# Stacked scores in the second attention, and the last output projections token tile by token tile

## The chip, the cores and the metric

The kernel runs on one core of a Trainium2 chip. The metric is the device time of one execution in microseconds, as the median of several runs. The kernel before takes 2476.68 us (three runs, 2473.72 to 2478.02).

A core has a matrix engine (TensorE, PE in the profile, with its weight loads apart as PEld), three engines for elementwise work (VectorE or DVE, ScalarE or ACT, GpSimd or POOL) and SyncE (SP), which here only issues DMAs. Each runs its own queue of instructions in order and waits for the others by semaphores.

## The reference

512 tokens of 1024 features go through two blocks in float32. The first block has a convolution branch, an attention and a feed-forward layer; the change does not touch it. The second block has two layers: one with the second attention, one with a state-space model (SSM), each followed by a feed-forward layer (FFN) with a short convolution. Cut to what the change touches:

```python
def attn_layer(h, w_in, w_out, ...):
    qa, ka, va, qb, kb, vb = jnp.split(h @ w_in, cuts, axis=-1)
    qa, ka = rmsnorm(heads(qa, H_A), q_norm_a), rmsnorm(heads(ka, H_A), k_norm_a)
    oa = band_attention(qa, ka, heads(va, H_A), A_PREV_CHUNKS, bias_a, None)
    qb, kb = rmsnorm(heads(qb, H_B), q_norm_b), rmsnorm(heads(kb, H_B_KV), k_norm_b)
    ob = band_attention(qb, kb, heads(vb, H_B_KV), B_PREV_CHUNKS, bias_b, sinks)
    return jnp.concatenate([oa, ob], axis=-1) @ w_out

def ssm_layer(h, w_in, ...):
    ...
    y = ssd_scan(xs, dt, a, bm, cm) + d_skip[:, None] * xs
    y = y.reshape(b, s, D_INNER) * jax.nn.silu(z)
    ...                      # normed in 4 groups of 512 features
    return y @ w_out

for layer in range(2):
    x = x + (attn_layer if layer == 0 else ssm_layer)(rmsnorm(x, norm_mix[layer]))
    x = x + conv_ffn(rmsnorm(x, norm_ffn[layer]))
```

The second attention has 8 heads of kind a (each with its own keys, a table of relative positions as bias) and 8 of kind b (two key heads, a slope times the distance as bias, and a sink). A head has 64 features.

## The kernel before

**Tiling.** Tokens go in four tiles (tt) of 128, features in k slices of 128. A float32 product is made of three fp32r matmuls, `mm3` (L390): both operands are split into a rounded part and the rest (names ending in h and l, or hi and lo), and hi x hi, hi x lo and lo x hi are added up in one PSUM bank. Weights come by DMA and are split in chunks of 512 columns (whi by ACT, wlo by DVE), at most nine ahead. In `jobA` (tile ga) the output has features on partitions and all 512 tokens move; in `jobB` and `projB` (tile gb) a token tile is the stationary operand, and the inner loop is over k. An output of 1024 columns is made in two halves of 512.

**What sets the order.** A planner in the Python program writes the instructions of all engines in one order. `run_jobs` (L355) goes through the list of projections (jobs); each yields every two k slices, and then `pump` runs whatever other work is due by the planner's own clocks: `spawn` and `step` hold generators with due times, `Flow` (L263) sends units of work through stages with given gaps (`LA` for the second attention, `SD` for the SSM). So small matmuls of attention or SSM are mixed into the stream of gb and ga matmuls, and all engines keep the order written. There are eight PSUM banks, and scratch tiles of 128x512 in a ring.

**The second attention** (`attn`). The projections come in the order kb and vb, qb, ka, qa, va. `head_norm` norms a token tile of one of them: squares (sq, on ACT), a sum, a power on GpSimd (ar), the product (ay, on DVE), transposes (at), and an eviction on ACT with the gain as scale (qb, ka, ... with the features of two heads on the 128 partitions). kb is written twice side by side, once for each half of the partitions, and needs four transposes a tile. `units_of` makes 64 units of scores, kind b first, for each token tile four pairs of heads (pr) and two heads (g) in a pair. The stages: sz copies q with the other head's half set to zero (`by_head`, L206; tile qz, on DVE or ACT, whichever the planner finds free sooner); s0 makes the score as one fp32 matmul (tile as; 128, 256, 384 or 512 keys in kind a, 128 or 256 in kind b) and then adds the bias and finds the least in one DVE instruction (`less`; tile ae); s1 and s2 are the exponential and the division; s3 transposes (ap, apT); s4 multiplies with the values (ao) and splits the output into oTh and oTl. For kind b the bias is one tile with the eight slopes multiplied in (relB8, eight ACT instructions).

**The first attention** already makes its scores (tile z) from stacked operands: hi and lo of a head lie on the two halves of the partitions, and two fp32r matmuls give the sum of all products. The halves are brought to the other partitions by DMAs that ACT issues (L1079).

**The output projections.** At the attention's end L1517 to L1523 put four jobs of 4 k slices: wo rows 512 and on (kind b) for column half 0 and 1, then rows 0 to 511 (kind a) for half 0 with all four token tiles, then half 1. When both halves and both kinds of a token tile are added to x, x is transposed (tr), scaled by the gain (xg) and split (hh, hl): that feeds the FFN's ga. The SSM has four groups. For the last, `outp(3, True)` (L1894) waits in the planner until the last token tile of y is normed and transposed (S[3, 3]), and then puts half 0 of all token tiles and then half 1. Before that each token tile's y goes through y matmuls, `join` (four DVE operations), a square on ACT, yr (DVE and GpSimd), a scaling on DVE, four transposes (yT) and the split into yTh and yTl.

## Time and profile before

| | |
|---|---|
| median of three runs | 2476.68 us |
| the profiled execution | 2474.39 us |
| its span | 2472.7 us, so 1.7 us lie around it |
| PE, PEld busy | 2432.4 us, 1975.4 us |
| DVE, ACT, POOL busy | 1527.4 us, 1113.9 us, 215.0 us |
| second attention, first to last score | 1164.4 to 1340.0 us |
| its end: FFN's first ga | 1362.1 us |
| SSM's end: FFN's first ga | 2118.3 us |

How to read it: a busy share of 98% means that hardly any of the span is left without a matmul in flight, but matmuls overlap, so what one costs is read from its start to the start of the next. The page's chain follows back from the last instruction what released what. Timelines and windows give microseconds from the start of the span.

### The profile page before, as it was taken

The numbers are of one execution on the slowest core, as the hardware profiler recorded it, in microseconds if no ns is written. First come the engines' busy times: TensorE is split into PE (matmuls) and PEld (weight loads), VectorE is DVE, ScalarE is ACT, GpSimd is POOL, SyncE is SP. The second block draws the span as 40 slices with busy tenths as digits, with TensorE's granted clock in tenths as the row PEclk, the third lists the DMA queues.
The fourth block names the chain that finished last, engine by engine and source line by source line (L and its number), as shares of the span: only waits on it lengthen the run. The fifth ranks groups of instructions, "written<-read, shape, count | busy, mean of one in ns | idle before, by whom it ended". The sixth has DMA issues, their size and how long they took to land.

```text
span 2472.7 us, 30712 instructions
## 1 busy us (share of the span) xinstructions
PE 2432.4 (98%) x11556; PEld 1975.4 (80%) x11556; DVE 1527.4 (62%) x2808; ACT 1113.9 (45%) x2406; POOL 215.0 (9%) x279
## 2 busy tenths in 40 slices
PE   8999999999999999999998999999999999999999
PEld 6877877788888888888776888888778887888887
DVE  6436466653434566656756666776698687667674
ACT  6545444432333445545666333333565635433332
POOL 1102011101110011102100000000000000001010
PEclk9999999999999999999999999999999999999999
DMA  5323332333323565622221354442432431345442
GB/s 208 103 59 95 111 100 80 88 109 111 99 89 119 153 163 144 120 91 82 68 87 35 104 143 120 131 107 80 118 107 77 124 115 60 97 142 119 137 111 77
DMA packets 218533, 264.78 MB, mean 107 GB/s; under 512 B 7024, under 2 KB 157936, under 8 KB 218384
## 3 DMA queue, kind: packets, MB, share of 16 engines
q1 hardware_dynamic: 198848, 222.83, 27.8%
q0 software_dynamic: 15232, 29.36, 7.4%
q10 hardware_dynamic: 4304, 10.62, 1.5%
q8 instruction: 91, 1.49, 0.3%
q14 instruction: 58, 0.48, 0.1%
HBM read 254.33 MB, written 4.26 MB: 105 GB/s over the span
## 4 chain that ended last, share of the span: by engine, by line
PE 87%; DVE 6%; issue 4%; ACT 1%; DMA 1%; POOL 0%; ACTq 0%; SPq 0%; POOLq 0%; DVEq 0%
PE ga L87 47%; PE gb L87 21%; PE gw L87 11%; PE y L87 1%; PE as L87 1%; DVE wlo L120 1%; DVE fy L120 1%; PE o L87 1%; PE tr L92 1%; PE aT L92 1%; PE z L87 1%; PE ao L87 1%; PE ap L92 1%; DVE ae L120 0%; DVE y L120 0%
## 5 line engine op out<-in xcount | busy, mean ns | idle before, releaser
L87 PE MATMUL ga<-hh,whi 128*128 128x512 f32 x1672 | 661.4, 396 | 0.0
L87 PE MATMUL ga<-hh,wlo 128*128 128x512 f32 x1672 | 651.8, 390 | 0.3 <-DVE wlo L120 0.2
L87 PE MATMUL ga<-hl,whi 128*128 128x512 f32 x1672 | 651.3, 390 | 0.0
L120 DVE TENSOR_TENSOR wlo<-raw,whi 128x512 fp32r<-128x512 f32 x701 | 479.3, 704 | 227.6 <-ACT whi L120 226.5
L120 ACT CAST whi<-raw 128x512 fp32r<-128x512 f32 x701 | 412.8, 617 | 156.8 <-PE ga L87 62.5
L87 PEld LDWEIGHTS ga<-hh,wlo 128*128 128x128 f32 x1672 | 313.2, 187 | 67.7 <-DVE wlo L120 1.2
L87 PEld LDWEIGHTS ga<-hh,whi 128*128 128x128 f32 x1672 | 313.4, 187 | 66.3 <-issue 3.0
L87 PEld LDWEIGHTS ga<-hl,whi 128*128 128x128 f32 x1672 | 313.6, 188 | 64.9 <-issue 1.7
L87 PE MATMUL gb<-whi,hh 128*128 128x512 f32 (+1 forms) x416 | 171.6, 412 | 0.0
L87 PE MATMUL gb<-wlo,hh 128*128 128x512 f32 (+1 forms) x416 | 159.3, 383 | 2.3 <-DVE wlo L120 2.2
L87 PE MATMUL gb<-whi,hl 128*128 128x512 f32 (+1 forms) x416 | 159.8, 384 | 0.0
L120 DVE TENSOR_TENSOR wlo<-b,whi 128x512 fp32r<-128x512 f32 x196 | 131.2, 686 | 36.9 <-ACT whi L120 36.9
L120 ACT ACTIVATE fy<-fy,cols 128x512 f32<-128x512 f32 x60 | 43.5, 726 | 202.1 <-DVE fy L120 200.4
L120 ACT CAST whi<-b 128x512 fp32r<-128x512 f32 x196 | 114.1, 616 | 15.6 <-PE gw L87 11.2
L120 DVE SCALAR_TENSOR_TENSOR x<-gw,rsp,x 128x512 f32<-128x512 f32 x98 | 70.0, 750 | 69.3 <-PE gw L87 69.2
L120 DVE SCALAR_TENSOR_TENSOR fy<-fg,cols,fy 128x510 f32<-128x510 f32 (+1 forms) x136 | 102.1, 751 | 4.8
L120 DVE TENSOR_TENSOR fg<-ga,R 128x512 f32<-128x512 f32 x68 | 46.9, 690 | 78.6 <-PE ga L87 67.2
L87 PEld LDWEIGHTS gb<-wlo,hh 128*128 128x128 f32 x416 | 78.6, 189 | 17.6 <-DVE wlo L120 3.7
L87 PEld LDWEIGHTS gb<-whi,hl 128*128 128x128 f32 x416 | 78.2, 188 | 16.0
L87 PEld LDWEIGHTS gb<-whi,hh 128*128 128x128 f32 x416 | 78.4, 188 | 14.6 <-issue 1.7
L655 POOL DMA_DIRECT2D b<-in_ffn_w_out_dram x32 | 38.5, 1205 | 507.6 <-DVE wlo L120 503.6
L87 PE MATMUL gw<-whi,fss 128*128 128x512 f32 x256 | 81.4, 389 | 0.0
(316 smaller groups left out, 3958.7 us busy)
## 6 DMA issues: line engine op xcount, KB each, us to landing
raw<-in_ffn_w_in_dram SPq DMA_DIRECT2D x44, 1024.0 KB, 5.1
raw<-in_w_in_dram SPq DMA_DIRECT2D x32, 1024.0 KB, 5.0
raw<-in_w_up_dram SPq DMA_DIRECT2D x16, 1024.0 KB, 5.4
b<-in_ffn_w_out_dram POOLq DMA_DIRECT2D x32, 512.0 KB, 5.7
raw<-in_ssm_w_in_dram SPq DMA_DIRECT2D x16, 1024.0 KB, 5.3
b<-in_w_down_dram POOLq DMA_DIRECT2D x24, 512.0 KB, 6.0
b<-in_ffn_w_out_dram SPq DMA_DIRECT2D x12, 1024.0 KB, 7.6
b<-in_w_down_dram SPq DMA_DIRECT2D x9, 1024.0 KB, 7.7
```

What stands on the lines that cost most here:

```text
L87: nc.tensor.matmul(o, lhsT=lhsT, rhs=rhs, **kw)
L92: nc.tensor.transpose(o, i, idn)
L120: return fn(*args, **kw)
L655: nc.gpsimd.dma_start(out=r3(R[nm][:, a * 512:(c + 1) * 512], c + 1 - a), in_=dram(i, j, a, c + 1), accum_op=ALU.add)
```

## The change

It has two parts. In the second attention q and k of both kinds are split into hi and lo, which lie on the two halves of the partitions. `queries` makes the tile qq of a token tile: a cast on ACT (hi) and a difference on DVE (lo) for each half of the partitions, and a DMA issued by GpSimd that copies both to the other half. `put_k` writes kb and ka as pairs of tiles. A score is two fp32r matmuls (`score`) in the place of one fp32 matmul. qz, `halves`, the doubled kb and relB8 go; the slope is taken into q's norm and `less` has a scale. Second, `projC` puts the attention's last output projection and the SSM's last one as two jobs whose weights are both kept (`Job.keep`): for each token tile half 0 and then half 1. The SSM's waits in the planner only for token tile 0 (S[3, 0]).

```diff
+            if j.keep:
+                continue
             st["used"] -= len(split.pop(i))
+            if i and jobs[i - 1].keep:
+                st["used"] -= len(split.pop(i - 1))
...
+    def projC(wap, r0, nk, X, evac, pre=None):
+        def run(w):
+            ws = (W(w.i - 1), w)
+            x = X()
+            quota[0] = 2
+            for tt in range(NT):
+                for half in range(2):
+                    ps = bank("g", "gb")
+                    for k in range(nk):
+                        wh, wl = ws[half].get(k, 0, 512)
+                        xh, xl = x.rd(k, tt * 128, tt * 128 + 128)
+                        mm3(ps, xh, xl, wh, wl, k == 0, k == nk - 1)
...
+                    hand_over()
+                    evac(half)(tt, ps)
...
+        def put_k(key):
...
+                    act.activation(out=t[hi, :, c], in_=ps[hi], func=AF.Copy, scale=gain)
+                    dve.scalar_tensor_tensor(out=t[lo, :, c], in0=ps[hi], scalar=gain, in1=f(t[hi, :, c]),
+                                             op0=ALU.mult, op1=ALU.subtract)
...
+        def queries(kind, tt):
+            while ("q" + kind, tt) not in S:
+                yield 0.3
+            t = u8("qq", F32R)
+            q = r3(S["q" + kind], 4)[:, :, tt * 128:tt * 128 + 128]
+            for g in range(2):
+                hi, lo = slice(64 * g, 64 * g + 64), slice(64 - 64 * g, 128 - 64 * g)
+                a = g * 1024
+                act.copy(r3(t[:, a:a + 512], 4)[hi], q[hi])
+                dve.tensor_sub(r3(t[:, a + 512:a + 1024], 4)[hi], q[hi], f(r3(t[:, a:a + 512], 4)[hi]))
+                nc.gpsimd.dma_start(out=t[lo, a:a + 1024], in_=t[hi, a:a + 1024])
+            yield 3.0
+            S["qq" + kind, tt] = t
...
+        def score(ps, q, k, pr, g):
+            for i in range(2):
+                o = g * 1024 + i * 512 + pr * 128
+                pe.matmul(ps, lhsT=q[:, o:o + 128], rhs=k, start=i == 0, stop=i == 1)
...
+                            if g == 0 and pr == 0 and tt == 0:
+                                spawn(queries(kind, 0))
+                            if g == 0 and pr == 2 and tt < 3:
+                                spawn(queries(kind, tt + 1))
...
-        for half in range(2):
-            jobB(wo, 0, 4, half * 512, O, 0, {}, True, True, residual(half),
-                 pre=(lambda: hooks.update(x=hooks["next2"])) if half == 0 else None)
+        projC(wo, 0, 4, O, residual, lambda: hooks.update(x=hooks["next2"]))
...
-                until(lambda: (g, 3) in S)
+                until(lambda: (g, 0 if last else 3) in S)
...
+            if last:
+                projC(wo, g * 512, 4, lambda: S["yT", g], residual, pre)
+                return
```

Three places where the order of instructions moves. **The first scores of kind b.** On GpSimd's queue, before, the powers ar of the token tiles follow one another:

```order
L120 TENSOR_TENSOR ar_9931<-ar_9931,mhalf_77 128x8
L120 TENSOR_TENSOR ar_9962<-ar_9962,mhalf_77 128x8
L120 TENSOR_TENSOR ar_10007<-ar_10007,mhalf_77 128x8
L120 TENSOR_TENSOR ar_10264<-ar_10264,mhalf_77 128x8
```

and now two DMAs (x2, one for each half of the partitions) stand between those of the third and the fourth token tile:

```order
L121 TENSOR_TENSOR ar_9931<-ar_9931,mhalf_77 128x8
L121 TENSOR_TENSOR ar_9962<-ar_9962,mhalf_77 128x8
L1409 DMA qq_9984<-qq_9984 64x1024 x2
L121 TENSOR_TENSOR ar_10003<-ar_10003,mhalf_77 128x8
L1409 DMA qq_10022<-qq_10022 64x1024 x2
```

On TensorE, before, the first score comes after two k slices of a projection:

```order
L92 MATMUL at_9974<-ident_75,ay_9941 128x128 x4
L87 MATMUL gb_9987<-whi108_0_9857,hh0_9322 128x512
L87 MATMUL gb_9987<-wlo108_0_9858,hh0_9322 128x512
L87 MATMUL gb_9987<-whi108_0_9857,hl0_9323 128x512
L87 MATMUL gb_9987<-whi108_1_9880,hh0_9322 128x512
L87 MATMUL gb_9987<-wlo108_1_9881,hh0_9322 128x512
L87 MATMUL gb_9987<-whi108_1_9880,hl0_9323 128x512
L87 MATMUL as_10000<-kbT_9633,qz_9984 128x128
```

and now (names with other numbers, the same work):

```order
L93 MATMUL at_10013<-ident_75,ay_9972 128x128 x4
L88 MATMUL gb_10029<-whi108_0_9857,hh0_9317 128x512
L88 MATMUL gb_10029<-wlo108_0_9858,hh0_9317 128x512
L88 MATMUL gb_10029<-whi108_0_9857,hl0_9318 128x512
L88 MATMUL gb_10029<-whi108_1_9880,hh0_9317 128x512
L88 MATMUL gb_10029<-wlo108_1_9881,hh0_9317 128x512
L88 MATMUL gb_10029<-whi108_1_9880,hl0_9318 128x512
L88 MATMUL as_10039<-kb_9637,qq_9984 128x128 x2
L88 MATMUL as_10045<-kb_9637,qq_9984 128x128 x2
L88 MATMUL as_10051<-kb_9637,qq_9984 128x128 x2
```

The first score has moved behind the next projection bank, and three scores stand in a row.

**The attention's end.** TensorE before, from the transposes (tr) of token tile 2, half 1, to the FFN's first ga:

```order
L92 MATMUL tr_12290<-ident_75,x1_6530 128x128 x4
L87 MATMUL gb_12282<-whi117_2_11811,oTh0_11370 128x512
L87 MATMUL gb_12282<-wlo117_2_11812,oTh0_11370 128x512
L87 MATMUL gb_12282<-whi117_2_11811,oTl0_11371 128x512
L87 MATMUL gb_12282<-whi117_3_11925,oTh0_11370 128x512
L87 MATMUL gb_12282<-wlo117_3_11926,oTh0_11370 128x512
L87 MATMUL gb_12282<-whi117_3_11925,oTl0_11371 128x512
L87 MATMUL ga_12310<-hh0_11832,whi118_0_12053 128x512
L87 MATMUL ga_12310<-hl0_11833,whi118_0_12053 128x512
```

and now, from the transposes of token tile 3, half 0:

```order
L93 MATMUL tr_12319<-ident_75,x1_6525 128x128 x4
L88 MATMUL gb_12309<-whi117_2_11766,oTh0_11400 128x512
L88 MATMUL gb_12309<-wlo117_2_11767,oTh0_11400 128x512
L88 MATMUL gb_12309<-whi117_2_11766,oTl0_11401 128x512
L88 MATMUL gb_12309<-whi117_3_11770,oTh0_11400 128x512
L88 MATMUL gb_12309<-wlo117_3_11771,oTh0_11400 128x512
L88 MATMUL gb_12309<-whi117_3_11770,oTl0_11401 128x512
L93 MATMUL tr_12342<-ident_75,x1_6525 128x128 x4
L88 MATMUL ga_12341<-hh0_11858,whi118_0_11783 128x512
L88 MATMUL ga_12341<-hl0_11859,whi118_0_11783 128x512
L88 MATMUL ga_12341<-hh0_11858,wlo118_0_11784 128x512
```

Both halves of the last token tile are now transposed directly ahead of ga, where before half 1 of the last token tile came after the first twelve ga.

**The SSM's end.** TensorE before, where y of token tile 3 (y1 with xdt, y2 with stt), the transposes of y of tiles 1 to 3 (yT) and the start of the last group's projection (whi185) stand:

```order
L87 MATMUL gb_18112<-whi184_3_17971,yTh0_17372 128x512
L87 MATMUL gb_18112<-wlo184_3_17972,yTh0_17372 128x512
L87 MATMUL gb_18112<-whi184_3_17971,yTl0_17373 128x512
L87 MATMUL y1_18162<-xdt_18000,m_17907 128x64 x4
L87 MATMUL y1_18162<-xdt_18000,m_17909 128x64 x4
L87 MATMUL y2_18171<-stt_18024,bc_17381 128x512
L92 MATMUL yT_18185<-ident_75,y_18015 128x128 x4
L92 MATMUL yT_18199<-ident_75,y_18081 128x128 x4
L92 MATMUL yT_18207<-ident_75,y_18133 128x128 x4
L87 MATMUL gb_18212<-whi185_0_17987,yTh0_18143 128x512
L87 MATMUL gb_18212<-wlo185_0_17988,yTh0_18143 128x512
L87 MATMUL gb_18212<-whi185_0_17987,yTl0_18144 128x512
```

and now, first where the last projection starts, right behind the one ahead of it:

```order
L93 MATMUL yT_18172<-ident_75,y_17930 128x128 x4
L88 MATMUL gb_18149<-whi184_2_17975,yTh0_17409 128x512
L88 MATMUL gb_18149<-wlo184_2_17976,yTh0_17409 128x512
L88 MATMUL gb_18149<-whi184_2_17975,yTl0_17410 128x512
L88 MATMUL gb_18149<-whi184_3_18008,yTh0_17409 128x512
L88 MATMUL gb_18149<-wlo184_3_18009,yTh0_17409 128x512
L88 MATMUL gb_18149<-whi184_3_18008,yTl0_17410 128x512
L88 MATMUL gb_18211<-whi185_0_18024,yTh0_18180 128x512
L88 MATMUL gb_18211<-wlo185_0_18025,yTh0_18180 128x512
L88 MATMUL gb_18211<-whi185_0_18024,yTl0_18181 128x512
```

then fifteen matmuls on, where y of token tile 3 and the transposes of token tile 1 stand:

```order
L88 MATMUL y1_18242<-xdt_18037,m_17944 128x64 x4
L88 MATMUL y1_18242<-xdt_18037,m_17946 128x64 x4
L88 MATMUL y2_18251<-stt_18061,bc_17418 128x512
L93 MATMUL tr_18253<-ident_75,x0_6524 128x128 x4
L88 MATMUL gb_18235<-whi186_2_18203,yTh0_18180 128x512
L88 MATMUL gb_18235<-wlo186_2_18204,yTh0_18180 128x512
L88 MATMUL gb_18235<-whi186_2_18203,yTl0_18181 128x512
L88 MATMUL gb_18235<-whi186_3_18207,yTh0_18180 128x512
L88 MATMUL gb_18235<-wlo186_3_18208,yTh0_18180 128x512
L88 MATMUL gb_18235<-whi186_3_18207,yTl0_18181 128x512
L93 MATMUL tr_18284<-ident_75,x0_6524 128x128 x4
L93 MATMUL yT_18297<-ident_75,y_18052 128x128 x4
```

The twelve transposes in a row are spread out, and the projection of token tile 0 stands ahead of y of token tile 3. On DVE, before, all four yTl come between the operations of y and the first x of this projection:

```order
L120 SCALAR_TENSOR_TENSOR y_18015<-y_18015,yr_18158,nw_17693 128x512
L120 TENSOR_TENSOR y_18133<-y1_18162,y_18133 128x512
L120 TENSOR_TENSOR yo_18178<-y2_18171,tok_87 128x512
L120 TENSOR_TENSOR y_18133<-y_18133,yo_18178 128x512
L120 TENSOR_TENSOR y_18133<-y_18133,sz_17815 128x512
L120 TENSOR_SCALAR yr_18182<-yms_18174 128x1
L120 TENSOR_TENSOR yTl0_18144<-yT_18185,yTh0_18143 128x4x128
L120 SCALAR_TENSOR_TENSOR y_18081<-y_18081,yr_18182,nw_17693 128x512
L120 TENSOR_SCALAR yr_18196<-yms_18193 128x1
L120 SCALAR_TENSOR_TENSOR y_18133<-y_18133,yr_18196,nw_17693 128x512
L120 TENSOR_TENSOR yTl0_18144<-yT_18199,yTh0_18143 128x4x128
```

and now the join of token tile 3 (y with y1, yo, y, y with sz), xg, rs and hl stand ahead of yTl of token tile 1:

```order
L121 SCALAR_TENSOR_TENSOR y_18052<-y_18052,yr_18195,nw_17730 128x512
L121 TENSOR_TENSOR x0_6524<-gb_18235,x0_6524 128x512
L121 TENSOR_TENSOR y_18170<-y1_18242,y_18170 128x512
L121 TENSOR_TENSOR yo_18276<-y2_18251,tok_86 128x512
L121 TENSOR_TENSOR y_18170<-y_18170,yo_18276 128x512
L121 TENSOR_TENSOR y_18170<-y_18170,sz_17852 128x512
L121 TENSOR_SCALAR yr_18280<-yms_18263 128x1
L121 TENSOR_TENSOR xg_18291<-tr_18284,cols_80 128x512
L121 TENSOR_SCALAR rs_18231<-ms_18230 128x1
L121 TENSOR_TENSOR hl0_18259<-xg_18260,hh0_18258 128x4x128
L121 TENSOR_TENSOR yTl0_18181<-yT_18297,yTh0_18180 128x4x128
```

## Rows read from the trace of the kernel before

**Rows 1.** The profile's page: the span, its part 1 (busy time, share of the span, instructions), the clock row of part 2, and the first row of part 4.

```profile
span 2472.7 us, 30712 instructions
...
PE 2432.4 (98%) x11556; PEld 1975.4 (80%) x11556; DVE 1527.4 (62%) x2808; ACT 1113.9 (45%) x2406; POOL 215.0 (9%) x279
...
PEclk9999999999999999999999999999999999999999
...
PE 87%; DVE 6%; issue 4%; ACT 1%; DMA 1%; POOL 0%; ACTq 0%; SPq 0%; POOLq 0%; DVEq 0%
```

**Rows 2.** The timeline of TensorE in two stretches of the second attention, one with scores of 256 columns and one with 512 (start us, us, engine, line, operation, count).

```profile
1247.96 0.60 PE L87 MATMUL as<-kbT,qz 128*128 128x256 f32 x2
1248.39 0.27 PE L92 MATMUL ap<-ident,ae 128*128 128x128 f32 x1
...
1320.99 1.02 PE L87 MATMUL as<-ka,qz 128*128 128x512 f32 x2
1321.85 0.27 PE L92 MATMUL ap<-ident,ae 128*128 128x128 f32 x1
```

**Rows 3.** The same view in the first attention: its scores z, 256 columns twice and 512 once, each followed by the next matmul.

```profile
212.73 0.48 PE L87 MATMUL z<-kk,qq 128*128 128x256 f32 x2
213.05 0.39 PE L87 MATMUL ga<-oxh,whi 128*128 128x512 f32 x1
...
293.00 0.40 PE L87 MATMUL z<-kk,qq 128*128 128x256 f32 x2
293.23 0.28 PE L92 MATMUL aT<-ident,a 128*128 128x128 f32 x1
...
520.88 0.62 PE L87 MATMUL z<-kk,qq 128*128 128x512 f32 x2
521.34 0.39 PE L87 MATMUL ga<-hh,whi 128*128 128x512 f32 x1
```

**Rows 4.** The view of the tile qz: its writers on DVE and ACT (duration in ns min/median/max, first and last start), and who waited for it (us, times).

```profile
L120 DVE TENSOR_SCALAR qz<-qb,halves x21: 267/279/286, 1163.9 to 1238.1; 128x128 f32<-128x128 f32 x21
...
L120 ACT ACTIVATE qz<-qb,halves x11: 386/397/420, 1196.6 to 1241.5; 128x128 f32<-128x128 f32 x11
...
  PE as L87: 2.0, 3
```

**Rows 5.** The view of the tile qq of the first attention: cast, difference, and the time from ACT's issue of the copy (256 KB) to its landing.

```profile
L120 ACT ACTIVATE qq<-ga x16: 591/592/594, 195.6 to 489.2; 64x512 fp32r<-64x512 f32 x16
L120 DVE SCALAR_TENSOR_TENSOR qq<-ga,qq x16: 682/688/695, 196.2 to 489.8; 64x512 fp32r<-64x512 f32 x16
...
DMA to landing us min/median/max: 2.8/2.9/2.9
```

**Rows 6.** The view of the tile b, whose loads of 512 KB GpSimd issues in the feed-forward layers: duration of an issue, and from issue to landing.

```profile
L655 POOL DMA_DIRECT2D b<-in_w_down_dram x24: 1203/1203/1371, 826.1 to 1044.3; - x24
...
DMA to landing us min/median/max: 5.5/5.8/7.2
```

**Rows 7.** The timeline of all engines where the first score of the second attention starts.

```profile
1163.21 0.69 ACT L120 ACTIVATE qb<-at,cols 128x512 f32<-128x512 f32 x1 [1.96 <-PE at L92]
...
1164.41 0.42 PE L87 MATMUL as<-kbT,qz 128*128 128x128 f32 x2
...
1166.11 2.09 POOL L120 TENSOR_TENSOR ar<-ar,mhalf 128x8 f32<-128x8 f32 x1 [1.62 <-DVE ar L120]
```

**Rows 8.** Busy time of each engine in a stretch of the second attention (us and instructions, for PE, PEld, DVE, ACT, POOL), then the granted clock, DMA share and GB/s.

```profile
1200.00:1250.00 50.00, 49.73 (x292) 38.64 (x291) 34.91 (x140) 37.37 (x121) 8.24 (x5) 1.00 0.20 64
```

**Rows 9.** What TensorE waited for at the end of the second attention (1318 to 1362 us) and of the SSM layer (2078 to 2127 us): us in total, times, longest; and between the two TensorE's timeline where the first ends.

```profile
PE gb L87 <- DVE oTl L120: 2.5, 3, 1.7
PE gb L87 <- ACT oTh L120: 2.2, 3, 1.0
...
1362.12 0.39 PE L87 MATMUL ga<-hh,whi 128*128 128x512 f32 x1
...
1364.84 0.60 PE L92 MATMUL tr<-ident,x 128*128 128x128 f32 x4
...
PE yT L92 <- DVE y L120: 5.9, 3, 3.0
```

**Rows 10.** The chain of waits through the end of the SSM layer, in order of time: start us, us, what.

```profile
2071.23 4.13 PE gb L87 x18
2075.36 2.65 PE y L87 x18
...
2081.79 0.70 DVE y L120
...
2090.54 1.11 PE yT L92 x4
2091.65 5.61 PE gb L87 x18
2097.26 0.44 PE tr L92 x4
...
2126.91 0.91 PE R L87 x8
```

**Rows 11.** Busy time of each engine (as in rows 8) in the hole at the end of the SSM layer and behind it.

```profile
2084.00:2095.00 11.00, 6.66 (x21) 5.16 (x22) 6.25 (x11) 3.00 (x6) 1.10 (x2) 0.53 0.01 1
2095.00:2128.00 33.00, 33.00 (x166) 27.38 (x165) 22.89 (x42) 14.76 (x34) 2.58 (x4) 1.00 0.19 64
```

More of the change, by code (lines that the diff above doesn't have):

```diff
@@ L68, in __init__ @@
         self.ahead = None
+        self.keep = False
 @with_exitstack
@@ L222 @@
     one = cp.tile([128, 1], F32, tag="one", name="one")
-    halves = cp.tile([128, 2], F32, tag="halves", name="halves")
     cols = cp.tile([128, NCOLS], F32, tag="cols", name="cols")
@@ L232, in setup_consts @@
         pool.memset(one, 1.0)
-        for i in range(2):
-            dve.memset(halves[64 * i:64 * i + 64, i:i + 1], 1.0)
-            dve.memset(halves[64 - 64 * i:128 - 64 * i, i:i + 1], 0.0)
         dve.memset(onesf, 1.0)
@@ L538, in projB @@
             n += m
+    def projC(wap, r0, nk, X, evac, pre=None):
[10 more added lines that the diff above has]
+                        mm3(ps, xh, xl, wh, wl, k == 0, k == nk - 1)
+                        if tt == NT - 1:
+                            w.done()
+                        if k % 2 and k + 1 < nk:
+                            yield
+                    hand_over()
+                    evac(half)(tt, ps)
+                    rel("t")
+                    yield
+        for half in range(2):
+            jobs.append(Job([(0, 512, wap[r0:r0 + nk * 128, half * 512:(half + 1) * 512])], nk, 512,
+                            run if half else lambda w: (), None if half else pre))
+        jobs[-2].keep = True
     SEVEN = (
@@ L1315, in attn, with less @@
         oT = {}
-        def less(e, s, bias, first, m):
-            dve.tensor_tensor_reduce(out=e, in0=s, in1=bias, scale=-1.0, scalar=first, op0=ALU.add, op1=ALU.min,
+        def less(e, s, bias, first, m, scale=1.0):
+            dve.tensor_tensor_reduce(out=e, in0=s, in1=bias, scale=-scale, scalar=first, op0=ALU.add, op1=ALU.min,
                                      accum_out=m)
         def load_rel():
-            relB = t2("relB")[:, 0:256]
+            relB = S["relB"] = cp.tile([128, 256], F32, tag="relB", name="relB")
             act.dma_start(out=relB, in_=ins["relB"])
@@ new lines, in queries @@
+        def queries(kind, tt):
[3 more added lines that the diff above has]
+            q = r3(S["q" + kind], 4)[:, :, tt * 128:tt * 128 + 128]
+            for g in range(2):
+                hi, lo = slice(64 * g, 64 * g + 64), slice(64 - 64 * g, 128 - 64 * g)
+                a = g * 1024
[4 more added lines that the diff above has]
+            S["qq" + kind, tt] = t
@@ L1421, in s0 @@
                                     load_bias(0)
-                                k = S["ka"][:, pr * 512:pr * 512 + n]
-                                pe.matmul(S_, lhsT=q, rhs=k, start=True, stop=True)
+                                k = S["ka"][g][:, pr * 512:pr * 512 + n]
+                                score(S_, q, k, pr, g)
                                 far = max(0, n - 256)
@@ L1430, in s0 @@
                             else:
-                                o = (pr // 2) * 512 + t0 * 128
-                                pe.matmul(S_, lhsT=q, rhs=S["kb"][:, o:o + n], start=True, stop=True)
-                                less(e, S_, S["relB"][:, h * 256 + 256 - n:h * 256 + 256], S["sink"][:, h:h + 1], m)
+                                score(S_, q, S["kb"][pr // 2][:, t0 * 128:t0 * 128 + n], pr, g)
+                                less(e, S_, S["relB"][:, 256 - n:256], S["sink"][:, h:h + 1], m, 2.0 ** -(h + 1))
                                 S["b left"] -= 1
@@ L1485, in units_of @@
                         s0.need, s3.need, s4.need = ("t", 1), ("t", 1), ("t", g)
+                        s0.when = lambda tt=tt: ("qq" + kind, tt) in S
                         sz.when = lambda tt=tt: ("q" + kind, tt) in S and ("k" + kind, tt) in S
```

74 lines of the change are left out of this document (32 added, 42 removed).

## The prediction

> **What bounds the kernel now.** I read the page first. TensorE is busy for 98% of the span and holds 87% of the chain that ended last, and its clock is granted in full in nearly every slice [rows 1]. So a change pays only where it takes matmul time away or fills a hole in front of a matmul, and everything below is counted on TensorE: what is issued less, and what it waits for more or less. Next come the timelines of one score in both forms of the arithmetic [rows 2, 3], the views by tile of what goes and what comes [rows 4 to 6], the start of the second attention [rows 7], the load of the other engines there [rows 8], the waits at its end [rows 9], and the chain through the end of the SSM layer with its clock [rows 10, 11].
>
> **Scores, removed and added.** A score now is one fp32 product. From the start of one to the start of the next matmul the reader sees 1248.39 - 1247.96 = 0.43 us at 256 columns and 1321.85 - 1320.99 = 0.86 at 512 [rows 2]. The first attention already has the stacked form, two fp32r matmuls into one bank, and takes 293.23 - 293.00 = 0.23 at 256 and 521.34 - 520.88 = 0.46 at 512 [rows 3]. A score therefore saves 0.20 at 256 and 0.40 at 512. At 384 I take 0.20 too, and at 128 nothing, since two short matmuls have little left to save. The second attention has 48 scores of 256 columns in as<-kbT, of which each fp32 one is two records, so 24, and 8 more in kind a; 8 of 384; 8 of 512; the rest are of 128. That makes (24 + 8) x 0.20 + 8 x 0.20 + 8 x 0.40 = 6.4 + 1.6 + 3.2 = 11.2 us. Four transposes fewer for kb are another 4 x 0.11 = 0.4 (a group of four takes 0.44 in the chain [rows 10]). If the pair at 256 takes 213.05 - 212.73 = 0.32, the longest that I found [rows 3], the 6.4 become 3.5 and the sum 8.3; that is the lower end of this term.
>
> **Scores, on the other engines.** Out go 37 qz copies on DVE of 0.28 and 27 on ACT of 0.39 [rows 4], some 10.4 and 10.5 us, and eight relB copies on ACT. In come 16 casts of 0.59 on ACT and 16 differences of 0.69 on DVE for qq [rows 5], 9.5 and 11.0 us, and the hi and lo parts of ka and kb, 16 evictions on each of the two. Net DVE gets some 3 to 7 us more over about 180 us, ACT about as much as before. Between 1200 and 1250 us both are under three quarters busy [rows 8], so I cost this at nothing on the path. What goes with qz are TensorE's waits for it, 2.0 us in 3 places [rows 4]; against that I set as much again, because every matmul now comes 0.2 us sooner to the same DVE and ACT results. Ends: 2 us gained, 4 us lost.
>
> **The copies.** Sixteen DMAs of 256 KB, issued by GpSimd. Of four token tiles three are asked for four units of scores ahead, about 11 us, and hidden. The first of kind b is not. In the row of before, qb ends on ACT at 1163.21 + 0.69 = 1163.9 and the first score starts at 1164.41 [rows 7]. After the change sq and the two casts follow on ACT (to 1165.5), two differences on DVE (to 1165.7 and 1166.3), then the two issues one after the other on GpSimd, 1.2 us each by the other DMAs that it issues [rows 6], then the landing. How long a 256 KB copy from GpSimd takes no row shows. The nearest from below is the same copy issued by ACT, 2.9 us [rows 5]; from above 512 KB issued by GpSimd, 5.8 [rows 6]. I take 4, between the two and a little nearer the first, whose size it has: halves land at 1169.7 and 1170.9. TensorE has moved its first score behind eighteen more matmuls and reaches it at about 1167.65. So it stands for 3.0 us; with 2.9 it is 2.0 and with 5.8 it is 5.0. Behind the score in TensorE's queue stand the projection matmuls that could have filled the hole, and behind the two issues in GpSimd's queue stands the ar power of the fourth token tile, now 1.6 to 2.1 us at 1166.11 [rows 7], which gets 1 to 2 us later and has slack.
>
> On GpSimd's DMAs the row shows 1203 ns at the median and 1371 at most over 24 of them, while DVE runs beside them [rows 6]. The Trainium skill (SBUF — State Buffer, section "SBUF: two separate sides") says that a DMA issued from GpSimd can be held up while VectorE runs an operation that takes both ports, because the descriptors can't be written, and that one issued from ACT or SP is immune. By that rule each of the two issues waits for a DVE instruction more, the stall is some 1.4 us longer, and the forecast would be 2474.8. The trace so far speaks against it: issue times hardly spread.
>
> **The attention's end.** The last output projections (wo rows 0 to 511) now go token tile by token tile, both halves of each. The waits there are 2.5 us for oTl and 2.2 for oTh [rows 9]. With both column halves of a token tile in a row there are twice the matmuls before the next oT is wanted, so most of these go: I keep 1.0 of the 4.7 for oT. What is late next is the FFN's first stage. Its first 24 ga want column half 0 of all tokens, the next 24 half 1. Now half 0 is long done when ga starts at 1362.12, and the last transposes, of half 1, stand at 1364.84 with twelve ga behind them that don't need them [rows 9]. Afterwards half 0 of the last token tile is transposed only six gb ahead of ga, and xg, the next tile's xg, hh and hl run in the open: by hand 2.5. Net 4.7 - 1.0 - 2.5 = 1.2 us gained; ends 3.7 gained (the boundary is free) and 2 lost (the FFN's weights, also on DVE, come late too).
>
> **The SSM's end.** This is the term that I am least sure of. Now yT waits three times for DVE's y chain, 5.9 us in all [rows 9]: DVE works on y around 2081.79, and gb goes on only at 2091.65, behind the last transposes [rows 10]. The projection then runs without a hole to R at 2126.91. After the change it starts as soon as yT of token tile 0 is there, and the y of tile 3 is issued in the middle of it, 18 matmuls later. I followed DVE's queue by its order and 0.70 for an operation of 512 columns that needs the one before it [rows 10], 0.1 less otherwise. Token tile 0: its yTl stands behind the join of tile 2 and is written at 2083.9, so gb stalls 3.8 us; 16 matmuls follow to 2087.6; y of tile 3 takes 2.6 [rows 10] to 2090.2; then transposes and six gb to 2092.1. Tile 1: yTl now stands behind x, the four operations of join 3, yr, xg, rs and hl, and is written at 2097.6: 5.1 us of stall. Tile 2: it is ready at 2107.3, 2.9 of stall. Tile 3: about 1. Then the last x, the last transposes and hl in front of ga: 2.8. R comes at 2132.7, 5.8 us later than now. Now the clock falls to the lower of its two levels (1.2 of 2.4 GHz) once, behind the first hole, for most of 2084 to 2095 [rows 11], so that 18 gb take 5.61 instead of 4.13 [rows 10], 1.5 us that the 5.8 do not contain; whether it falls again no row tells, so I add half of that, 0.7. Cost 6.5. Ends: all that is lost now is won, the 5.9 of waits and some 2 of half clock, 8 us gained; or five holes with 1.5 us of half clock each, 5.8 + 7.5 = 13 lost.
>
> **The sum.** 11.2 + 0.4 - 3.0 + 1.2 - 6.5 = 3.3 us gained. The profiled execution took 2474.39 us (its span 2472.7 and 1.7 around it), so it would be 2471.1; the median of before is 2476.68, 2.3 above the profiled one, and I forecast 2473.4.
>
> **The rivals.**
> - The SSM's end goes as its order means it to: DVE gets yTl out early enough, and the holes are the short ones. For it: TensorE has 33 us of work in this stretch and DVE 23 [rows 11]. Against: DVE runs in order, and join 3 now stands in front of yTl of tile 1. Then the 6.5 lost become 4 gained, half of the best: 2463.
> - It gets slower: half clock. TensorE's many holes at the SSM's end (some 15 us in 45) pull the clock to 0.5 as the hole of now does, and five holes cost 1.5 each. The term is then -13.3, not -6.5, and the sum 11.2 + 0.4 - 3.0 + 1.2 - 13.3 = 3.5 lost; with 5.0 for the first scores and 2 lost at the attention's end it is 8.7. I take the middle, 2483. It decides from about 9 us lost at the SSM's end. For it: 0.53 on average from 2084 to 2095 [rows 11]. Against: the holes are shorter, with matmuls between them.
> - The scores' gain is not kept: DVE and ACT set the pace of a unit, and what TensorE saves turns into waits for ae and apT. For it: ACT is busy 37 of 50 us [rows 8] and all stages of a unit lie on these two. Against: TensorE is busy 49.7 of these 50. Then 7 of the 11.6 are lost: 2480.
> - The change does less than it says, if the pair at 256 costs 0.32: 2476.3, inside the forecast's own range.
>
> **How the numbers follow.** Forecast 0.43, own range 2468 to 2479; SSM's end filled 0.20; slower by half clock 0.20; scores' gain lost 0.17. The measurement can tell 0.2%, 5.0 us, from no change: under 2471.7 is faster, over 2481.6 slower. Faster: 0.20 + 0.17 of the forecast's 0.43, whose middle lies a little inside, = 0.37. Slower: 0.15 of the half clock's 0.20 and 0.05 of the lost scores' 0.17 = 0.20. The rest, 0.43, is no change. From 2462 to 2483 leaves out the outer halves of the first two rivals, 0.2.
>
> **What would show it.** Right: a score of 512 columns takes 0.46; as waits for qq once, about 3 us near 1168, and for no other; the waits for oTl and oTh shrink to one; ga waits some 2.5 for hl at the end of either layer; gb waits for yTl at the SSM's end four times, 3 to 5 us. Wrong: the holes at the SSM's end sum to under 8 us (then the order works), or qq is waited for at every token tile, or the granted clock is at half over more than the 11 us of now.

## The result, and the profile after

The changed kernel takes 2491.63 us (2491.22 to 2496.08, four runs) against 2476.16 of the kernel before: a ratio of 1.0067, 95% interval 1.0052 to 1.0082. It is slower by 15.5 us; the forecast was 2473.4, with 2483 as the slow end.

The page's span and first part answer to [rows 1]. TensorE is busy 2 us less, in a span that is 17.6 us longer:

```profile
span 2490.3 us, 30712 instructions
...
PE 2430.2 (98%) x11552; PEld 1976.2 (79%) x11552; DVE 1535.4 (62%) x2787; ACT 1119.7 (45%) x2403; POOL 223.8 (9%) x303
```

Marks split these 17.6 us. R stands at each FFN's start and at the SSM's, eight matmuls each time, and the view of the tile R gives the first start (behind the second attention) and the last (behind the SSM), before and after:

```profile
L87 PE MATMUL R<-dg,onesf x24: 270/275/275, 1370.8 to 2127.5; 128*128 128x128 f32 x24
...
L88 PE MATMUL R<-dg,onesf x24: 270/275/276, 1375.0 to 2143.8; 128*128 128x128 f32 x24
```

So 4.2 us are lost up to the attention's end, (2143.8 - 1375.0) - (2127.5 - 1370.8) = 12.1 from there up to the SSM's end, and 1.3 behind it. The R at the SSM's start, at 1724.1 before and 1729.7 now, splits the 12.1: 1.4 in the FFN behind the attention, 10.7 in the SSM. I had expected 9.8 gained at the first mark and 5.8 to 6.5 lost at the second.

What TensorE waited for in the second attention, 1160 to 1390 us (us in all, times, longest). Before, it stood 8.2 us there, of which the rows for oT and qz in [rows 4, 9] are 6.7; now the list is of other things (its nine longest rows):

```profile
PE as L88 <- DMA qq<-qq: 4.1, 4, 1.6
PE ap L93 <- ACT apT L121: 3.0, 2, 2.4
PE gb L88 <- ACT apT L121: 2.5, 1, 2.5
PE tr L93 <- DVE x L121: 2.2, 2, 1.4
PE ap L93 <- ACT ae L121: 1.9, 3, 1.1
PE ga L88 <- DVE wlo L121: 1.5, 1, 1.5
PE gb L88 <- ACT oTh L121: 1.2, 2, 0.8
PE ga L88 <- ACT hh L121: 1.1, 1, 1.1
PE ga L88 <- DVE hl L121: 0.9, 1, 0.9
```

And at the SSM's end, 2078 to 2145 us, where before one row of 5.9 us stood [rows 9]:

```profile
PE gb L88 <- DVE yTl L121: 7.5, 4, 3.6
PE gb L88 <- ACT yTh L121: 1.8, 2, 1.1
PE tr L93 <- DVE x L121: 1.6, 2, 0.8
PE ga L88 <- ACT hh L121: 1.1, 1, 1.1
PE ga L88 <- DVE hl L121: 0.9, 1, 0.9
```

The clock adds to the holes. Windows of the after run (us, then busy time with its count for PE, PEld, DVE, ACT and POOL, granted clock, DMA share, GB/s), first of the attention (it answers to [rows 8]), then of the SSM's end ([rows 11]):

```profile
1200.00:1250.00 50.00, 43.05 (x251) 32.77 (x249) 37.18 (x121) 36.33 (x107) 10.77 (x9) 0.97 0.22 64
```

```profile
2084.00:2095.00 11.00, 7.37 (x25) 5.66 (x23) 6.99 (x12) 2.68 (x7) 0.55 (x1) 0.69 0.36 120
2095.00:2128.00 33.00, 26.22 (x127) 19.99 (x127) 18.66 (x33) 9.93 (x24) 2.89 (x5) 0.95 0.00 0
2128.00:2145.00 17.00, 14.19 (x59) 11.04 (x58) 6.84 (x15) 5.02 (x11) 1.16 (x2) 0.90 0.19 62
```

In 1200 to 1250 TensorE is busy 43.05 us where it was 49.73, and the clock is below 1, which it never was there before. Where it falls, it falls to the lower level (1.2 of 2.4 GHz), behind a hole. I added up over windows of 2 us what stood still (holes) and, as an estimate, what was lost at the lower level ((1 - granted clock) x busy time):

| 1160 to 1390 us | holes | lost by the clock | R of the attention's end, after the last gw<-whi,ffs of the first block |
|---|---|---|---|
| before | 8.2 | 0.0 | 306.8 |
| changed | 20.6 | 3.3 | 311.2 |
| scores_only | 20.5 | 7.4 | 317.0 |
| scores_reorder | 20.8 | 3.1 | 313.0 |
| stacked_a | 18.2 | 6.6 | 318.1 |
| stacked_b | 12.4 | 3.3 | 310.2 |

The last column fixes the work. Of the changed kernel's 20.6 us of holes 1.5 (the wait for wlo) lie behind this R, before 0.1; so up to R it has 11.0 + 3.3 = 14.3 us more of holes and clock, but R comes only 4.4 later, and matmul work worth 9.9 us is gone. The same account gives 9.4 to 9.6 for scores_only and scores_reorder, and 8.6 to 12.2 over all kernels below that make each score of both kinds once in the stacked form, so it is good to some 2 us. My sum had 11.6. Most of the work was saved; it went into holes.

### The profile page after: what moved, and what is told of

It reads as the page before. It is cut to its first block, busy times and chain, and to the rows that moved or that the text cites. A ratio compares the mean times of both kernels' runs of the same rounds, so it can differ in the third digit from the quotient of the medians.

```text
span 2490.3 us, 30712 instructions
## 1 busy us (share of the span) xinstructions
PE 2430.2 (98%) x11552; PEld 1976.2 (79%) x11552; DVE 1535.4 (62%) x2787; ACT 1119.7 (45%) x2403; POOL 223.8 (9%) x303
## 5 line engine op out<-in xcount | busy, mean ns | idle before, releaser
L121 ACT CAST whi<-b 128x512 fp32r<-128x512 f32 x196 | 114.2, 616 | 15.6 <-PE gw L88 11.2
```

Source lines behind the costliest of these rows:

```text
L121: return fn(*args, **kw)
```

## The experiments

Each set is timed beside the kernel before on one chip, where that takes 2474 to 2475 us; each number is a median. Executions of one kernel differ by some us (scores_reorder took 2478.98 to 2486.00), and a trace shows one of them. "Base" is a kernel of the second set.

**The parts.** The changed kernel with the old code at one or both ends, and with put_k written in another order:

```diff
 scores_only, scores_att_c, scores_reorder
-                projC(wo, g * 512, 4, lambda: S["yT", g], residual, pre)
+                (the two projB of the kernel before, until (g, 3) in S)
 scores_only, scores_reorder
-        projC(wo, 0, 4, O, residual, lambda: hooks.update(x=hooks["next2"]))
+        (the two jobB of the kernel before)
 scores_reorder, changed_reorder
-   for g: act hi(g); dve lo(g)
+   act hi(0); act hi(1); dve lo(0); dve lo(1)
```

> The stacked scores alone; both last output projections as in the kernel before. Theory A (most of the 17 us lost come from the SSM's end, 12.5 by the shift of its R against its first yT, and the rest from the second attention's scores): 2478 to 2481 us, two to five slower than before, with the 2.4 and 2.5 us waits for apT still there. Theory B (token tile by token tile at the attention's end is what costs there): equal to before or up to 5 us faster, 2471 to 2476.

> The changed kernel with the SSM's end as before. Theory A: 12 to 13 us under the changed kernel, 2478 to 2480, and the SSM's end has the one hole of before. A rival (the loss at the SSM's end is made earlier, by work that the attention pushes back): the time falls by less than 8, to 2484 or more.

> As scores_only, but put_k writes hi of both key halves on ACT first and then lo of both on DVE. Theory A1 (the lockstep ACT, DVE, ACT, DVE over one PSUM bank holds up both queues, 3.0 us per ka tile, and TensorE's 4.9 us of waits for apT come from it, and the half clock behind them): 5 to 7 us under scores_only, so 2472 to 2475. Rival A2 (ACT and DVE are too busy with the stacked form whatever the order): within 2 us of scores_only.

> The changed kernel with put_k reordered in the same way. A1: 5 to 7 us under the changed kernel, 2485 to 2487. A2: within 2 us of it, 2490 to 2493.

| | us | ratio to before | 95% interval |
|---|---|---|---|
| scores_only | 2485.44 | 1.0041 | 1.0027 to 1.0055 |
| scores_att_c | 2481.05 | 1.0023 | 1.0014 to 1.0033 |
| scores_reorder | 2481.76 | 1.0028 | 1.0019 to 1.0037 |
| changed_reorder | 2491.74 | 1.0070 | 1.0054 to 1.0085 |

The SSM's end costs 2491.63 - 2481.05 = 10.6 us (9.4 if each is taken against the kernel before of its own set), a little under theory A; the stacked scores alone cost 10.5, twice what it had for them; and the attention's end gains 4.4 beside them. Theory B falls. The reorder gains 3.7 at the median where only the scores are changed, with overlapping runs, and nothing in the changed kernel. In the traces it shortens no holes (20.5 and 20.8 us; waits for apT 4.6 and 3.9); the difference is in the clock (7.4 and 3.1). So A1 is not shown: it names where holes lie, not what their sum comes from.

What A1 is about is seen in the after trace at 1203 us. On ACT (start, us, operation, in brackets the idle time before it and what ended it):

```profile
1202.95 1.25 ACT L121 CAST qq<-qb 64x512 fp32r<-64x512 f32 x2
1204.22 0.62 ACT L121 CAST whi<-raw 128x512 fp32r<-128x512 f32 x1
1204.74 0.68 ACT L121 ACTIVATE ka<-at,cols 64x512 fp32r<-64x512 f32 x1
1206.23 0.68 ACT L121 ACTIVATE ka<-at,cols 64x512 fp32r<-64x512 f32 x1 [0.81 <-DVE ka L121]
1206.94 0.37 ACT L121 COPY apT<-ap 128x256 f32<-128x256 f32 x1
```

on DVE:

```profile
1203.59 1.40 DVE L121 TENSOR_TENSOR qq<-qb,qq 64x512 fp32r<-64x512 f32 x2 [0.29 <-ACT qq L121]
1205.45 0.74 DVE L121 SCALAR_TENSOR_TENSOR ka<-at,cols,ka 64x512 fp32r<-64x512 f32 x1 [0.46 <-ACT ka L121]
```

and on TensorE:

```profile
1207.36 0.44 PE L93 MATMUL ap<-ident,ae 128*128 128x128 f32 x2 [2.40 <-ACT apT L121]
```

Two casts of q and a weight stand in one block, then ka's hi, and the second hi waits 0.81 us for DVE's lo of the other half, though it needs nothing of it; both read one PSUM tile. The copy apT behind them starts at 1206.94, and TensorE stands 2.40 us for it. The next ka tile brings the same rows 5.2 us later, and behind them TensorE's longest hole here:

```profile
1211.44 0.68 ACT L121 ACTIVATE ka<-at,cols 64x512 fp32r<-64x512 f32 x1 [0.81 <-DVE ka L121]
1212.15 0.37 ACT L121 COPY apT<-ap 128x256 f32<-128x256 f32 x1
...
1212.57 0.50 PE L88 MATMUL gb<-whi,hh 128*128 128x512 f32 x1 [2.46 <-ACT apT L121]
```

The Trainium skill (PSUM — Partial Sum Buffer, section "PSUM bank collisions raise a hardware error") says that two engines must not touch one bank in the same quadrant of partitions at once, reads included, and that software keeps them apart. The two halves here lie in different quadrants, which by that page could be read together; so the rule does not ask for the wait of 0.81 us in the trace, and no run here shows what does. With the reorder the 0.81 is gone, but the four operations remain in front of the units' short ones.

**The copies, the planner's distances, the SSM's start.** Base is scores_att_c with put_k reordered.

```diff
 late_scores
-            yield 3.0
+            yield 7.0                      # queries: until qq may be used
 copies_on_act
-                nc.gpsimd.dma_start(out=t[lo, a:a + 1024], in_=t[hi, a:a + 1024])
+                act.dma_start(out=f(t[lo, a:a + 1024]), in_=f(t[hi, a:a + 1024]))
 spread_casts
+                if g == 0:
+                    yield 1.2, 0.1         # between the halves of queries
 eight_units, no_first_gap, longer_lags: LA
-(0.9, 0.2, (0.2, 0.1), (0.2, 1.5), (0.2, 1.2), 1.4, 6)
+6 -> 8;  0.9 -> 0.1;  1.5, 1.2 -> 2.3, 2.0
 ssm_order_only (base with projC at the SSM's end)
-                until(lambda: (g, 0 if last else 3) in S)
+                until(lambda: (g, 3) in S)
```

> Scores with put_k reordered, attention's end token tile by token tile, SSM's end as before. If the two effects add up (4.4 us by the attention's end, 3.7 by the order in put_k): 2477 to 2478 us. If the token-tile order covers the same waits as the reorder does (changed_reorder did not gain): 2480 to 2482.

> As base, but the planner counts 7 us instead of 3 until a tile of copies may be used, so that the first scores stand some 19 matmuls later in TensorE's queue. Theory C (the waits for the copies cost what they show, 4.1 us): 3 to 5 us under base, and no wait for qq. Rival C2 (what TensorE does not wait for here it waits for later, since ACT and DVE then get the units later): within 1.5 us of base.

> As base, but ACT issues the copies of q, as in the first attention, in the place of GpSimd. If the time to landing (3.6 us from GpSimd, 2.9 from ACT) is what counts: 1 us faster. If the issue blocks ACT's queue (0.47 us each, behind DVE's difference): same as base or up to 5 us slower, with more waits for apT and ae.

> As base, but the planner puts 1.2 us between the two halves of a tile of copies, so that the two casts of q (1.25 us in a row) no longer stand together in ACT's queue ahead of ae and apT. Theory F (the holes of the first 50 us come from such blocks in ACT's and DVE's queues): waits for apT and ae fall from 5.0 to under 3 us, the time to 2474 to 2478. Rival F2 (the sum of work on ACT and DVE makes them): within 1.5 us of base, and the waits go elsewhere.

> As base, with eight units of scores in flight in the plan instead of six. Theory E: the units go faster, the last score comes earlier against the projections' matmuls, and the holes at the attention's end shrink: 3 to 6 us under base, 2475 to 2478. Rival E2: same as base within 1.5 us. A third way (DVE and ACT are the bound, whatever is in flight): slower than base by more waits for ae and apT.

> As base, with the gap of 0.9 us between the first two stages of a unit cut to 0.1: it was for the copy qz, which is gone. Theory E: a unit is in flight for 0.8 us less of some 17, the pace is a twentieth faster: 1 to 4 us under base. Rival E2: same as base within 1.5 us.

> As base, but the planner leaves 0.8 us more before the transposes (ap) and before the product with the values (ao) of a unit, so that TensorE comes to them later in its queue. Theory G (TensorE now is ahead of ACT because a score costs it less, and the order must give ACT that time back): fewer waits for ae and apT, 2 to 4 us under base. Rival: the units take longer, six in flight, and what is won there is lost at the attention's end: same as base, or slower.

| | us | ratio to before | 95% interval | holes, clock, 1160 to 1390 us |
|---|---|---|---|---|
| base | 2480.38 | 1.0017 | 1.0008 to 1.0027 | 18.9, 6.4 |
| late_scores | 2478.77 | 1.0014 | 1.0005 to 1.0024 | 20.8, 3.0 |
| copies_on_act | 2488.32 | 1.0049 | 1.0032 to 1.0065 | 21.8, 10.5 |
| spread_casts | 2480.21 | 1.0022 | 1.0013 to 1.0032 | 18.6, 3.1 |
| eight_units | 2485.35 | 1.0037 | 1.0023 to 1.0050 | 21.6, 9.7 |
| no_first_gap | 2493.00 | 1.0070 | 1.0055 to 1.0085 | 26.0, 13.4 |
| longer_lags | 2496.71 | 1.0089 | 1.0075 to 1.0104 | 23.6, 15.2 |

Base is within 1 us of scores_att_c, so the 4.4 and the 3.7 do not add up. Late_scores has no wait for qq left (4.1 us in base) and is 1.6 us faster at best, its interval overlapping base's: TensorE now waits 4.9 us for oTh and 4.4 for as behind ay, which is close to rival C2. Copies_on_act is 8 us slower, although the wait for qq falls to 2.5: ACT, which issues them behind DVE's differences, delivers apT later (waits of 4.0, 2.5 and 1.0 us). GpSimd's issue is better here. Spreading the casts moves the waits (ay 2.3, ka 2.0) and wins nothing, as F2 says: the sum of work on ACT and DVE stays a rival to the blocks in their queues. Eight units, a shorter first gap and longer lags all lose, up to 16 us, with more holes and far more time at half clock: theories E and G fall, and with them my idea that one distance is wrong. What each run shows is that every order tried has its holes in other places. With the distances LA of base, both kinds stacked and each score made once, their sum stays at 18.6 to 21.8 us, and what differs most is the clock, 3.0 to 10.5.

**Is TensorE's time for a score free?** Scores_twice and old_price have the same order of instructions on every engine; the first makes each score twice.

```diff
 scores_twice
-            for i in range(2):
+            for i in (0, 1, 0, 1):
 old_price
+            now[0] += 2 * max(k.free_size() / 2400.0 + 0.003, 0.108)   # planner's clock alone
```

> As base, but every score is made twice over into the same bank (four fp32r matmuls, the second pair starts afresh), so TensorE has as much or more to do for scores as in the kernel before. The planner counts them. To be compared with old_price, which has the same order of instructions. Theory E (the second attention runs at the pace of its units, six in flight, and TensorE's time for a score is not what sets it): within 2.5 us of old_price. Rival E2 (TensorE's time decides): 7 to 9 us over old_price.

> As base, with nothing added to the chip's work, but the planner's clock counts a score as four short matmuls and not as two, so that its order is the one of scores_twice. Theory E: the order comes out nearer to that of the kernel before, with fewer matmuls of the projections ahead of the last scores: 1 to 4 us under base. Rival E2: same as base.

Scores_twice takes 2493.95 (1.0068, 1.0051 to 1.0085), old_price 2481.72 (1.0026, 1.0017 to 1.0036): 12.2 us apart. Up to R holes and clock are 14.2 + 8.1 against 17.1 + 9.6, and R comes 12.5 later: of 17.0 us of work added 4.5 go into holes and clock that were there, and three quarters show. Theory E falls, and the difference is above the 7 to 9 of E2: matmul time is not free here, and what a score saves would show for the most part if no new holes came with it.

**Which half, and what is worth keeping.** The kernel before with stacked scores for one kind alone (put_k reordered, both ends old), and with the attention's end alone:

```diff
 stacked_a: kind "a" with put_k("ka"), queries, score; kind "b" as before
 stacked_b: kind "b" with put_k("kb"), queries, score; kind "a" as before
 stacked_a_att_c, old_scores_att_c
-        (the two jobB of the kernel before)
+        projC(wo, 0, 4, O, residual, lambda: hooks.update(x=hooks["next2"]))
```

> The kernel before with stacked scores for kind a alone (put_k reordered, GpSimd's copies for a), kind b as before, both ends as before. If the holes come mostly with kind b (its first copies stand open, and its casts meet the norms of ka and qa on ACT): kind a saves 5 to 6 us of matmul time and loses little, 2470 to 2474, under before. If the ka pair and the tail make them: 2476 to 2482.

> The same for kind b alone. By the first reading most of the loss of scores_reorder (6.8 us) is here although kind b saves only 2 to 5 us: 2478 to 2483. By the second: 2474 to 2477.

> As stacked_a, with the attention's last output projection token tile by token tile. It gained 4.4 us beside the stacked scores and nothing beside the old ones. If it mends the waits for oT that stacked scores make longer: 2 to 4 us under stacked_a, and so the fastest of all. If stacked_a has no longer waits for oT: the same as stacked_a.

> The kernel before with one part of the change: the attention's last output projection token tile by token tile, the scores and the SSM's end as before. By the pair scores_only and scores_att_c that part is worth 4.4 us. If it is worth as much beside the old scores, whose waits for oT at the end are 4.7 us: 2470 to 2472, under both kernels. If it only mends waits that the stacked scores made worse (oTh 4.5, oTl 3.0 in scores_only): within 1.5 us of before.

| | us | ratio to before | 95% interval |
|---|---|---|---|
| stacked_a | 2483.45 | 1.0039 | 1.0024 to 1.0054 |
| stacked_b | 2475.83 | 1.0005 | 0.9996 to 1.0015 |
| stacked_a_att_c | 2485.37 | 1.0045 | 1.0030 to 1.0060 |
| old_scores_att_c | 2476.61 | 1.0006 | 0.9996 to 1.0015 |

The second reading is the nearer: kind a alone loses 9.0 us, somewhat over the 2476 to 2482 of that reading, and kind b costs nothing that can be told. But the parts do not add up, since kind a alone loses more than both kinds together (6.8 us in scores_reorder). By the table above kind a saves (18.2 - 8.2) + 6.6 - (318.1 - 306.8) = 5.3 us of work and pays 16.6 for it in the execution traced (2485.90, the longest of its four). One hole of stacked_a shows how. DVE:

```profile
1195.92 1.51 DVE L120 SCALAR_TENSOR_TENSOR ka<-at,cols,ka 64x512 fp32r<-64x512 f32 x2 [0.59 <-ACT ka L120]
1197.44 0.69 DVE L120 TENSOR_REDUCE am<-sq 128x8 f32<-128x512 f32 x1
...
1198.50 0.69 DVE L120 TENSOR_TENSOR ay<-gb,ar 128x512 f32<-128x512 f32 x1
1199.11 0.15 DVE L120 TENSOR_TENSOR sd<-sd,se 128x1 f32<-128x1 f32 x1
```

ACT:

```profile
1194.50 1.38 ACT L120 ACTIVATE ka<-at,cols 64x512 fp32r<-64x512 f32 x2
...
1199.55 0.51 ACT L120 ACTIVATE ae<-ae,sd 128x256 f32<-128x256 f32 x1 [2.85 <-DVE asc L120]
1199.96 0.68 ACT L120 ACTIVATE qz<-qb,halves 128x128 f32<-128x128 f32 x2
```

TensorE, and the same place before:

```profile
1200.40 0.70 PE L87 MATMUL as<-kbT,qz 128*128 128x256 f32 x2 [3.71 <-ACT qz L120]
...
1196.46 0.67 PE L87 MATMUL as<-kbT,qz 128*128 128x256 f32 x2 [0.89 <-DVE sd L120]
```

The two lo parts of ka (1.51 us) stand in DVE's queue ahead of the norm of the next tile (am, ay) and of two tiny sums sd. ACT's ae waits 2.85 us for those, qz stands behind ae, and TensorE, which passed this place before with a wait of 0.89 us, stands 3.71. Nothing is busy for long: an extra 1.5 us on one in-order queue, and the 0.59 that DVE stood for ka's hi before it, have gone through three engines. The changed kernel has no qz, so this hole is not one of its own; it shows how such a block spreads.

The attention's end is worth 4.4 us beside both kinds stacked, nothing beside stacked_a, nothing beside the old scores. I took it to mend waits for oT that stacked scores make long (4.5 and 3.0 us in scores_only), but stacked_a has them as long (4.4 and 3.0): with the new end they fall to 1.6 and 0.8, and x, hh and hl come to 3.3 + 1.1 + 0.9. Why it wins beside both kinds only stays open. Beside the old scores oTh falls from 2.2 to 1.2 us and oTl vanishes, and hh, hl, x and wlo in front of ga come to 1.2 + 0.9 + 0.8 + 1.5. None of the 18 kernels is faster than the kernel before.

**The SSM's end.**

> As base, but the SSM's last projection goes token tile by token tile, and starts in the plan only when all four token tiles of y are transposed, as in the kernel before. Theory D (the loss of 10 us comes from starting early: y of tile 3 behind the matmuls of tile 0 and yTl behind join in DVE's queue): equal to base within 3 us, the rest being the boundary to the FFN (hh and hl in front of ga, 2 us). Rival D2 (token tile by token tile is itself what costs): 8 us or more over base.

It takes 2487.74 us (1.0045, 1.0030 to 1.0060), 7.4 over base. Changed_reorder, which starts early as well, is 11.4 over base. So D2 is nearer: token tile by token tile itself costs 7.4, and the early start, meant to fill the hole, 4.0 more. Against base the trace has 2.8 us more of holes from 2070 us to the last R, 3.6 more of clock and 1.4 more of waiting for wlo behind R. The chain of ssm_order_only behind the hole (start us, us, what; [rows 10] is the same stretch before):

```profile
2122.18 1.41 PE gb L88 x6
...
2123.62 0.70 DVE x L121
...
2126.21 0.68 DVE xg L121
2126.90 0.61 DVE hl L121
...
2127.55 11.06 PE ga L88 x35
2138.61 0.91 PE R L88 x8
```

Between the last gb and ga lie x, xg and hl, 4 us in the open, and the 35 ga behind them take 11.06 us, since the clock is at half in that stretch (0.50 from 2128 to 2132); the changed kernel has the same chain and 9.80. Before, 36 ga took 2.72 + 5.49 with no wait, because the last transposes stood inside them.

## Why the prediction was wrong

**Right in the main.** The work: 11.6 us predicted, 9.9 by the account above, and less by the rows that I took it from. Two scores of the after run, 256 and 512 columns, each with the next matmul:

```profile
1224.81 0.48 PE L88 MATMUL as<-kb,qq 128*128 128x256 f32 x2
1225.12 0.40 PE L88 MATMUL gb<-whi,hh 128*128 128x512 f32 x1
```

and

```profile
1344.09 0.62 PE L88 MATMUL as<-ka,qq 128*128 128x512 f32 x2
1344.65 0.55 PE L88 MATMUL ao<-apT,va 128*64 128x128 f32 x6
```

That is 0.31 and 0.56 us, not 0.23 and 0.46 [rows 3]. Over all scores with no wait behind them the medians are 0.32, 0.44 and 0.56 us at 256, 384 and 512 columns, before 0.43, 0.64 and 0.90: by these the saving is 32 x 0.11 + 8 x 0.20 + 8 x 0.34 = 7.8 us. That is near the 8.3 which I gave as the lower end, with 0.32 for the pair at 256. The account by holes gives more; part of it is the transposes and what a score overlaps with its neighbours, and how much each is I did not separate. GpSimd's copies took 509 to 611 ns to issue and 3.6 us to land, where I had 1203 ns and 4:

```profile
L1409 POOL DMA_DIRECT2D qq<-qq x16: 509/518/611, 1165.7 to 1317.7; - x16
...
DMA to landing us min/median/max: 2.9/3.6/5.1
```

The first two waits for them are 1.6 and 1.0 us, 2.6 against 3.0; two more, 1.6 together, come at the first scores of kind a, which I had not counted. As in the trace before, GpSimd's issues hardly spread while DVE works beside them (it was busy for 74% of 1200 to 1250). So the 1.4 us that I weighed by the rule of the Trainium skill (SBUF — State Buffer, section "SBUF: two separate sides") do not show; whether DVE ran an operation that takes both ports meanwhile, no run here shows. The boundary at the attention's end: 2.5 by hand, 1.1 + 0.9 in the list, and with wlo 1.5.

**The step that failed first** is "Between 1200 and 1250 us both are under three quarters busy [rows 8], so I cost this at nothing on the path", with its ends of 2 gained and 4 lost. Measured: up to R 11.0 us more holes and 3.3 of clock in the changed kernel, of which I had counted 3.0 for the copies and 2.5 for the boundary. DVE and ACT were indeed 74% and 73% busy. But a share of busy time says how much work fits, not whether a short operation finds its queue free when TensorE needs it, and the change puts four operations of 0.7 us for each ka tile (one before) and four of 0.6 to 0.7 for each qq tile (in the place of the short copies qz) into the middle of a stream of units. The holes of 2.40 and 2.46 us lie behind such blocks. That blocks, and not the sum of work on the two engines, make the whole 11.0 is not shown: the reorder and spread_casts took blocks apart, and the holes only moved. The rival "the scores' gain is not kept" had this mechanism, but at 7 us and a chance of 0.17.

**The step mis-sized** is the SSM's end, "Cost 6.5". The chain by hand was right in its places: yTl of tile 1 behind x, the four of join 3, xg and hl. The after run's chain:

```profile
2099.03 0.69 DVE x L121
2099.73 0.60 DVE y L121
...
2102.44 0.60 DVE xg L121
...
2103.16 0.60 DVE hl L121
2103.76 0.61 DVE yTl L121
...
2104.41 5.24 PE gb L88 x16
```

I had it written at 2097.6, counting from a first yTl 4.1 us earlier (2083.9, here 2088.0); here it is 2104.4, and the other 2.7 us are the 16 gb between, which took 6.51 us mostly at the lower clock, where I had 3.7. The holes add up to 13.3 us from 2070 to 2150, before 6.1; my 15.6 of stalls was high. What was low is the clock: I gave 0.7 us to it, and 5.9 were lost, before 3.0. It fell three times (0.50 in 2088 to 2092, 0.50 in 2104 to 2106, 0.51 in 2136 to 2138): behind holes of 3.6 and 2.1 us, and behind three of 0.8 to 1.1. The FFN's weights come late too, which I had named as an end: ga waits 1.5 for wlo behind R, 0.2 before. The rival of half clock had the sign, the place and a price of 13.3 for this term, near the 10.7 + 1.3 measured; I gave it 0.20. That its price comes so near is in part luck. Changed_reorder has the same code at the SSM's end and the same 13.2 us of holes up to R, but lost only 1.5 to the clock there, and its SSM still takes 8.3 us longer than before. So most of that cost is there without the clock, which differs between these two traces.

**Right sign only:** the attention's end, 1.2 forecast, 4.4 beside both kinds of new scores and none beside the old.

What stays open: whether an order of the planner's exists in which the stacked scores keep their 10 us, and whether blocks or the sum of work on ACT and DVE make the holes. Six changes of distance and order were tried, none found it.

## What to carry to other kernels

In a kernel whose TensorE is full, do not cost a change on the other engines at nothing because they are three quarters busy: look for the longest block that it puts into an in-order queue ahead of something TensorE needs soon, and allow for the clock behind each hole. Taking one block out may only move the hole. An order that finishes all rows of one part before the next puts independent work between a result and its first use; turning the loop round to start earlier takes that work away, and the end of the stage is where it is missed.

## What I had not expected of the hardware

The clock cost as much as the added holes in one run: longer_lags lost 15.2 us to the lower level with 23.6 us of holes (8.2 before), late_scores only 3.0 with 20.8. So 2.8 us more of idle time came with 12.2 more of clock, and the two are 18 us apart; what in the order of the holes makes that, no run here shows. The issue of a copy of 64 x 1024 from SBUF by GpSimd took 0.51 us, that of a 512 KB load from HBM 1.20 [rows 6].
